# A variance over rows on one core: new tile order, last tiles shared between VectorE and ScalarE, loads split at the end, last stores from SyncE

## Chip, cores, metric

One core of one Trainium2 chip. The metric is device time in microseconds (us), median over runs. All runs compared here are of the fast state, but for one single look that is used for its trace alone.

Two words recur. A *packet* is one piece that one of the 16 DMA engines moves, 8 KB in a whole tile. A transfer has *landed* when all the DMA engines that took part in it are through, so that whoever waits for it may start.

## The reference

```python
x = np.random.randn(32, 512, 1024).astype(np.float32)
mean_sq = np.mean(x**2, axis=-1)
sq_mean = np.mean(x, axis=-1)**2
return mean_sq - sq_mean            # (32, 512): the variance of each of 16384 rows
```

67.1 MB are read, 64 KB are written.

## The kernel before

128 partitions; a tile is J = 2 rows of 1024 numbers in each partition, 1 MB, 64 tiles. Three of four tiles go to VectorE (statistics of two half rows, then an aggregate to mean and variance), one of four to ScalarE (one pass for the mean, one for the mean square, by accumulators). The order is D D D A, D for VectorE and A for ScalarE, so the very last tile is an A.

```python
J = 2; DV_FRAC = 3; XBUFS = 12; DV_CHUNK_COLS = 24; AC_CHUNK_COLS = 16
# ... cut: pools, order = D D D A, repeated

def flush_dv_chunk(lo, hi):
    res_dv = opool.tile([P, DV_CHUNK_COLS], fp32, name="res_dv")
    nc.vector.tensor_copy(out=res_dv[:, :n], in_=acc_dv[:, 1, lo:hi])          # L72
    nc.gpsimd.dma_start(out=out_t[:, lo:hi], in_=res_dv[:, :n])                # L73

def flush_ac_chunk(lo, hi):
    # tmp = mean * mean on VectorE (L79); res_ac = mean square - tmp (L83)
    nc.gpsimd.dma_start(out=..., in_=res_ac[:, :n])                            # L87

for t in order:
    xt = xpool.tile([P, J, 2, D // 2], fp32, name="xt")
    nc.sync.dma_start(out=xt, in_=src)                                         # L97
    if t < DV:
        for j in range(J):
            nc.vector.bn_stats(out=stats[:, j, 0, :], in_=xt[:, j, 0, :])      # L102
            nc.vector.bn_stats(out=stats[:, j, 1, :], in_=xt[:, j, 1, :])      # L103
            nc.vector.bn_aggr(out=acc_dv[:, :, t * J + j], in_=...)            # L104
        # ... cut: flush_dv_chunk every 24 columns
    else:
        for j in range(J):
            nc.scalar.activation(..., func=Copy, scale=1/D, accum_out=mean)            # L116
            nc.scalar.activation(..., func=Square, scale=D**-0.5, accum_out=mean_sq)   # L122
        # ... cut: flush_ac_chunk every 16 columns
```

## Time and profile before

| what | value | read from |
|---|---|---|
| time | 173.51 us (173.35 to 173.54) | runs |
| span of the profile | 171.6 us | head of the page |
| last load landed | 163.54 us | start of ScalarE's last tile in the timeline |
| VectorE, ScalarE busy | 129.1 and 74.8 us | part 1 of the page |
| DMA rate between start and tail | 416 to 428 GB/s | 40 slices |

The busy shares bound nothing here: the stream of loads runs at one rate from 5 to 161 us, and what can be won lies before and after it. The prediction shows the lines.

### The profile page before, as it was taken

How to read it: one execution, taken by the hardware profiler on the slowest of the kernel's cores; microseconds unless marked ns; L12 is line 12 of the kernel's file. 1: busy time of each engine (PE TensorE's matmuls, PEld its weight loads, DVE VectorE, ACT ScalarE, POOL GpSimd, SP SyncE). 2: the span in 40 equal slices, each digit the busy share in tenths (PEclk: the TensorE clock that was granted, in tenths of full speed). 3: DMA queues.
4: the chain of work that ended last, by engine and by line, in shares of the span. 5: the costliest groups of instructions: out<-in, count | busy, mean ns of one | idle time of the engine just before them, and what ended most of it. 6: DMA issues, size and time to landing. Idle time of an engine off the chain costs nothing.

```text
span 171.6 us, 597 instructions
## 1 busy us (share of the span) xinstructions
DVE 129.1 (75%) x296; ACT 74.8 (44%) x129; POOL 3.6 (2%) x10
## 2 busy tenths in 40 slices
DVE  0795959769695986959699793968969596995930
ACT  2009064280815528091642807346190824518082
POOL 0000000000100000000110000000010000000011
DMA  5999999999999999999999999999999999999600
GB/s 206 424 428 426 426 422 418 420 424 420 424 421 422 422 422 424 420 418 426 422 423 416 426 420 422 422 420 418 428 422 421 420 420 426 422 422 420 258 3 2
DMA packets 9412, 67.21 MB, mean 392 GB/s; under 512 B 1120, under 2 KB 1216, under 8 KB 1216
## 3 DMA queue, kind: packets, MB, share of 16 engines
q1 hardware_dynamic: 9216, 67.11, 94.0%
q0 software_dynamic: 192, 0.07, 0.2%
q14 instruction: 4, 0.03, 0.0%
HBM read 67.11 MB, written 0.07 MB: 392 GB/s over the span
## 4 chain that ended last, share of the span: by engine, by line
DMA 89%; DVE 5%; issue 3%; SPq 1%; POOLq 0%; POOL 0%
DMA xt<-in_x_dram 89%; DVE stats L102 2%; DVE stats L103 2%; SPq L97 1%; DVE acc_dv L104 1%; POOLq L157 0%; POOL out_dram L73 0%; DVE res_dv L72 0%
## 5 line engine op out<-in xcount | busy, mean ns | idle before, releaser
L102 DVE BATCH_NORM_STATS2 stats<-xt 128x6 f32<-128x512 f32 x96 | 64.1, 667 | 33.5 <-DMA xt<-in_x_dram 33.5
L116 ACT ACTIVATE garbage<-xt 128x1024 f32<-128x1024 f32 x32 | 33.8, 1057 | 91.7 <-DMA xt<-in_x_dram 91.2
L103 DVE BATCH_NORM_STATS2 stats<-xt 128x6 f32<-128x512 f32 x96 | 63.2, 658 | 0.0
L122 ACT ACTIVATE garbage<-xt 128x1024 f32<-128x1024 f32 x32 | 33.8, 1056 | 1.0
L104 DVE BATCH_NORM_AGGREGATE acc_dv<-stats 128x2 f32<-128x12 f32 x96 | 19.4, 202 | 1.6
L122 ACT ACTIVATION_READ_ACCUMULATOR garbage<-xt 128x1 f32 x32 | 6.0, 186 | 0.0
L116 ACT ACTIVATION_READ_ACCUMULATOR garbage<-xt 128x1 f32 x32 | 6.0, 186 | 0.0
L73 POOL DMA_DIRECT2D out_dram<-res_dv x4 | 2.3, 572 | 158.4 <-DVE res_dv L72 158.4
L79 DVE TENSOR_TENSOR tmp<-mean_ac 128x16 f32<-128x16 f32 x2 | 0.4, 176 | 3.0 <-ACT garbage L116 3.0
L116 ACT ACT_TABLE_LOAD x1 | 1.3, 1283 | 0.7 <-PEq L146 0.7
L87 POOL DMA_DIRECT2D out_dram<-res_ac x2 | 1.1, 538 | 7.1 <-DVE res_ac L83 7.1
L83 DVE TENSOR_TENSOR res_ac<-msq_ac,tmp 128x16 f32<-128x16 f32 x2 | 0.3, 166 | 1.0 <-ACT garbage L122 1.0
L72 DVE COPY res_dv<-acc_dv 128x24 f32<-128x24 f32 x4 | 0.7, 178 | 0.1
L146 POOL MEMSET const-float32-0.0<- 128x1 f32 x1 | 0.1, 98 | 0.2 <-issue 0.2
L146 POOL MEMSET const-bfloat16-1.0<- 128x1 bf16 x1 | 0.1, 101 | 0.0
L146 POOL MEMSET const-float32-1.0<- 128x1 f32 x1 | 0.1, 98 | 0.0
L146 POOL MEMSET const-uint8-127<- 128x1 uint8 x1 | 0.1, 98 | 0.0
## 6 DMA issues: line engine op xcount, KB each, us to landing
xt<-in_x_dram SPq DMA_DIRECT2D x64, 1024.0 KB, 19.8
out_dram<-res_dv POOLq DMA_DIRECT2D x4, 12.0 KB, 5.2
out_dram<-res_ac POOLq DMA_DIRECT2D x2, 8.0 KB, 3.3
```

The source lines that it names most:

```text
L72: nc.vector.tensor_copy(out=res_dv[:, :n], in_=acc_dv[:, 1, lo:hi])
L73: nc.gpsimd.dma_start(out=out_t[:, lo:hi], in_=res_dv[:, :n])
L79: nc.vector.tensor_tensor(out=tmp[:, :n], in0=mean_ac[:, lo:hi], in1=mean_ac[:, lo:hi], op=mybir.AluOpType.mult,)
L83: nc.vector.tensor_tensor(out=res_ac[:, :n], in0=msq_ac[:, lo:hi], in1=tmp[:, :n], op=mybir.AluOpType.subtract,)
L87: nc.gpsimd.dma_start(out=out_t[:, DV * J + lo:DV * J + hi], in_=res_ac[:, :n])
L97: nc.sync.dma_start(out=xt, in_=src)
L102: nc.vector.bn_stats(out=stats[:, j, 0, :], in_=xt[:, j, 0, :])
L103: nc.vector.bn_stats(out=stats[:, j, 1, :], in_=xt[:, j, 1, :])
L104: nc.vector.bn_aggr(out=acc_dv[:, :, t * J + j], in_=stats[:, j].rearrange("p a b -> p (a b)"),)
L116: nc.scalar.activation(out=garbage, in_=xt[:, j], func=mybir.ActivationFunctionType.Copy, scale=inv_d, accum_out=mean_ac[:, jt + j:jt + j ...
L122: nc.scalar.activation(out=garbage, in_=xt[:, j], func=mybir.ActivationFunctionType.Square, scale=inv_sqrt_d, accum_out=msq_ac[:, jt + j:j ...
L146: nc = _bacc.Bacc("TRN2", target_bir_lowering=False, num_devices=1)
```

## The change

It is meant to shorten what comes after the last load. The last A tile is shared: ScalarE takes one of its rows and VectorE the other, and so for one more tile two places before it. The last three tiles are loaded in rows, the last row in halves. A tiles now lead their groups instead of closing them. The last two stores are issued by SyncE. VectorE stores are read straight from the accumulators, without a copy. There are 16 tile buffers in place of 12.

```diff
-XBUFS = 12
+XBUFS = 16
-    for _ in range(DV_FRAC): ... D D D A ...
+    for g in range(n_act_groups):            # 13 groups: A, then 4 or 3 D
+        order.append((DV + g, False))
+        ...
+    order.append((A_last, False))
+    order.append((di, False)); di += 1
+    order.append((di, False)); di += 1
+    order.append((P_t, True))                # row 0 VectorE, row 1 ScalarE
+    order.append((Q_t, True))                # VectorE
+    order.append((R_t, True))                # row 0 ScalarE, row 1 VectorE
-        nc.vector.tensor_copy(out=res_dv[:, :n], in_=acc_dv[:, 1, lo:hi])
-        nc.gpsimd.dma_start(out=out_t[:, lo:hi], in_=res_dv[:, :n])
+        eng = nc.sync if final else nc.gpsimd
+        eng.dma_start(out=out_t[:, lo:hi], in_=acc_dv[lo // DV_CHUNK_COLS][:, 1, :])
+        if split:                            # P, Q, R
+            for j in range(J):
+                if t == R_t and j == 1:
+                    for u in range(2):
+                        nc.sync.dma_start(out=xt[:, j, u], in_=src[:, j, u])
+                else:
+                    nc.sync.dma_start(out=xt[:, j], in_=src[:, j])
+        elif t == R_t:
+            act_row(xt, 0, (t - DV) * J)
+            dve_row(xt, 1, None, special=15)     # variance straight into the tile `fin`
+            ac_cols(lo_f + 13, lo_f + 15, fin[:, 29:31], nc.vector)
+            nc.sync.dma_start(out=out_t[:, ...], in_=fin[:, 16:32])
# ... cut: the same for P with GpSimd; the middle ScalarE chunk's subtraction on GpSimd
```

More of the change, by code (lines that the diff above doesn't have):

```diff
@@ L9 @@
 J = 2
-DV_FRAC = 3
-XBUFS = 12
+XBUFS = 16
 DV_CHUNK_COLS = 24
@@ L29 @@
     T = N // (P * J)
-    if J == 1:
-        x_t = x.rearrange("b (u t) d -> t (b u) d", t=T)
-        out_t = out.rearrange("b (u t) -> (b u) t", t=T)
-    else:
-        x_t = x.rearrange("b (u t j) d -> t (b u) j d", t=T, j=J)
-        out_t = out.rearrange("b (u t j) -> (b u) (t j)", t=T, j=J)
-    DV = (T * DV_FRAC) // 4
+    x_t = x.rearrange("b (u t j) d -> t (b u) j d", t=T, j=J)
+    out_t = out.rearrange("b (u t j) -> (b u) (t j)", t=T, j=J)
+    DV = (T * 3) // 4
     AC = T - DV
@@ L44 @@
     opool = ctx.enter_context(tc.tile_pool(name="opool", bufs=8))
-    acc_dv = rpool.tile([P, 2, DV * J], fp32)
+    acc_dv = [rpool.tile([P, 2, DV_CHUNK_COLS], fp32, name=f"acc_dv{c}")
+              for c in range(DV * J // DV_CHUNK_COLS)]
     mean_ac = rpool.tile([P, AC * J], fp32)
@@ L51, with flush_dv, ac_cols @@
     inv_sqrt_d = float(D) ** -0.5
-    order = []
-    di, ai = 0, 0
-    while di < DV or ai < AC:
-        for _ in range(DV_FRAC):
-            if di < DV:
-                order.append(di)
-                di += 1
-        for _ in range(4 - DV_FRAC):
-            if ai < AC:
-                order.append(DV + ai)
-                ai += 1
-    assert sorted(order) == list(range(T))
+    n_act_groups = AC - 3
+    P_t = DV + AC - 2
+    R_t = DV + AC - 1
+    A_last = DV + AC - 3
+    d_total = DV
+    d_tail = 3
+    d_steady = d_total - d_tail
+    order = []
+    di = 0
+    for g in range(n_act_groups):
+        order.append((DV + g, False))
+        take = (d_steady + n_act_groups - 1 - g) // n_act_groups
+        for _ in range(take):
+            order.append((di, False))
+            di += 1
+    order.append((A_last, False))
+    order.append((di, False)); di += 1
+    order.append((di, False)); di += 1
+    Q_t = DV - 1
+    order.append((P_t, True))
+    order.append((Q_t, True))
+    order.append((R_t, True))
+    assert di == DV - 1
+    assert sorted(t for t, _ in order) == list(range(T))
     dv_cols_done = 0
     ac_cols_done = 0
-    def flush_dv_chunk(lo, hi):
-        res_dv = opool.tile([P, DV_CHUNK_COLS], fp32, name="res_dv")
-        n = hi - lo
-        nc.vector.tensor_copy(out=res_dv[:, :n], in_=acc_dv[:, 1, lo:hi])
-        nc.gpsimd.dma_start(out=out_t[:, lo:hi], in_=res_dv[:, :n])
-    def flush_ac_chunk(lo, hi):
+    def flush_dv(lo, hi, final=False):
+        eng = nc.sync if final else nc.gpsimd
+        eng.dma_start(out=out_t[:, lo:hi], in_=acc_dv[lo // DV_CHUNK_COLS][:, 1, :])
+    fin = rpool.tile([P, 32], fp32)
+    lo_f = AC * J - 16
+    def ac_cols(lo, hi, dst, eng):
         n = hi - lo
         tmp = opool.tile([P, AC_CHUNK_COLS], fp32, name="tmp")
-        res_ac = opool.tile([P, AC_CHUNK_COLS], fp32, name="res_ac")
-        nc.vector.tensor_tensor(
+        eng.tensor_tensor(
             out=tmp[:, :n], in0=mean_ac[:, lo:hi], in1=mean_ac[:, lo:hi],
@@ L82, in flush_ac_chunk, with flush_ac @@
         )
-        nc.vector.tensor_tensor(
-            out=res_ac[:, :n], in0=msq_ac[:, lo:hi], in1=tmp[:, :n],
+        eng.tensor_tensor(
+            out=dst, in0=msq_ac[:, lo:hi], in1=tmp[:, :n],
             op=mybir.AluOpType.subtract,
         )
-        nc.gpsimd.dma_start(
-            out=out_t[:, DV * J + lo:DV * J + hi], in_=res_ac[:, :n]
-        )
-    for t in order:
-        xt = xpool.tile([P, J, 2, D // 2], fp32, name="xt")
-        if J == 1:
-            src = x_t[t].rearrange("p (j u v) -> p j u v", j=J, u=2)
-        else:
-            src = x_t[t].rearrange("p j (u v) -> p j u v", u=2)
-        nc.sync.dma_start(out=xt, in_=src)
+    def flush_ac(lo, hi):
+        res_ac = opool.tile([P, AC_CHUNK_COLS], fp32, name="res_ac")
+        ac_cols(lo, hi, res_ac[:, :hi - lo], nc.gpsimd)
+        nc.gpsimd.dma_start(out=out_t[:, DV * J + lo:DV * J + hi],
+                            in_=res_ac[:, :hi - lo])
@@ new lines, in dve_row, with act_row @@
+    def dve_row(xt, j, col, special=None):
+        stats = spool.tile([P, 2, 6], fp32, name="stats")
+        nc.vector.bn_stats(out=stats[:, 0, :], in_=xt[:, j, 0, :])
+        nc.vector.bn_stats(out=stats[:, 1, :], in_=xt[:, j, 1, :])
+        dst = (fin[:, special:special + 17:16] if special is not None
+               else acc_dv[col // DV_CHUNK_COLS][:, :, col % DV_CHUNK_COLS])
+        nc.vector.bn_aggr(out=dst, in_=stats.rearrange("p a b -> p (a b)"))
+    def act_row(xt, j, col):
+        garbage = gpool.tile([P, 2, D // 2], fp32, name="garbage")
+        nc.scalar.activation(
+            out=garbage, in_=xt[:, j],
+            func=mybir.ActivationFunctionType.Copy,
+            scale=inv_d,
+            accum_out=mean_ac[:, col:col + 1],
+        )
+        nc.scalar.activation(
+            out=garbage, in_=xt[:, j],
+            func=mybir.ActivationFunctionType.Square,
+            scale=inv_sqrt_d,
+            accum_out=msq_ac[:, col:col + 1],
+        )
@@ new lines @@
+    for t, split in order:
+        xt = xpool.tile([P, J, 2, D // 2], fp32, name="xt")
+        src = x_t[t].rearrange("p j (u v) -> p j u v", u=2)
+        if split:
[5 more added lines that the diff above has]
+                    nc.sync.dma_start(out=xt[:, j], in_=src[:, j])
+        else:
+            nc.sync.dma_start(out=xt, in_=src)
@@ L99 @@
         if t < DV:
-            stats = spool.tile([P, J, 2, 6], fp32, name="stats")
             for j in range(J):
-                nc.vector.bn_stats(out=stats[:, j, 0, :], in_=xt[:, j, 0, :])
-                nc.vector.bn_stats(out=stats[:, j, 1, :], in_=xt[:, j, 1, :])
-                nc.vector.bn_aggr(
-                    out=acc_dv[:, :, t * J + j],
-                    in_=stats[:, j].rearrange("p a b -> p (a b)"),
-                )
-            dv_cols_done += J
-            if dv_cols_done % DV_CHUNK_COLS == 0 or dv_cols_done == DV * J:
-                lo = (dv_cols_done - 1) // DV_CHUNK_COLS * DV_CHUNK_COLS
-                flush_dv_chunk(lo, dv_cols_done)
-        else:
-            jt = (t - DV) * J
-            garbage = gpool.tile([P, 2, D // 2], fp32, name="garbage")
+                dve_row(xt, j, t * J + j)
@@ new lines @@
+            dv_cols_done += J
+            if dv_cols_done % DV_CHUNK_COLS == 0:
+                flush_dv(dv_cols_done - DV_CHUNK_COLS, dv_cols_done,
+                         final=(dv_cols_done == DV * J))
+        elif t == P_t:
+            dve_row(xt, 0, None, special=12)
+            act_row(xt, 1, (t - DV) * J + 1)
+            ac_cols(lo_f, lo_f + 12, fin[:, 16:28], nc.gpsimd)
+            ac_cols_done += J
+        elif t == R_t:
+            act_row(xt, 0, (t - DV) * J)
+            dve_row(xt, 1, None, special=15)
+            ac_cols_done += J
+            ac_cols(lo_f + 13, lo_f + 15, fin[:, 29:31], nc.vector)
+            nc.sync.dma_start(out=out_t[:, DV * J + lo_f:DV * J + AC * J],
+                              in_=fin[:, 16:32])
+        else:
@@ L115 @@
             for j in range(J):
-                nc.scalar.activation(
-                    out=garbage, in_=xt[:, j],
-                    func=mybir.ActivationFunctionType.Copy,
-                    scale=inv_d,
-                    accum_out=mean_ac[:, jt + j:jt + j + 1],
-                )
-                nc.scalar.activation(
-                    out=garbage, in_=xt[:, j],
-                    func=mybir.ActivationFunctionType.Square,
-                    scale=inv_sqrt_d,
-                    accum_out=msq_ac[:, jt + j:jt + j + 1],
-                )
+                act_row(xt, j, (t - DV) * J + j)
@@ L128 @@
             ac_cols_done += J
-            if ac_cols_done % AC_CHUNK_COLS == 0 or ac_cols_done == AC * J:
-                lo = (ac_cols_done - 1) // AC_CHUNK_COLS * AC_CHUNK_COLS
-                flush_ac_chunk(lo, ac_cols_done)
+            if ac_cols_done % AC_CHUNK_COLS == 0 and ac_cols_done < AC * J:
+                flush_ac(ac_cols_done - AC_CHUNK_COLS, ac_cols_done)
 _INS = ['x']
```

## The prediction

> **What bounds the kernel now.** I read the page from the top: the busy tenths, the DMA queues, the chain that ended last, and then the timeline of the end, because the chain turned out to follow a side branch there.
>
> ```profile
> DVE  0795959769695986959699793968969596995930
> ACT  2009064280815528091642807346190824518082
> DMA  5999999999999999999999999999999999999600
> GB/s 206 424 428 426 426 422 418 420 424 420 424 421 422 422 422 424 420 418 426 422 423 416 426 420 422 422 420 418 428 422 421 420 420 426 422 422 420 258 3 2
> ```
>
> From slice 2 to 37 the DMA engines are full and move 416 to 428 GB/s; VectorE and ScalarE both have holes. Then come about 2.5 slices of 4.29 us with no loads. So the time is three parts: a start, a stream of 67 MB at a fixed rate, and a tail. The change cannot remove bytes, so only the tail is worth anything.
>
> How deep the stream is queued is read from SyncE's own waits and from the issues:
>
> ```profile
> SPq L97 <- DMA xt<-in_x_dram: 117.2, 56, 3.0
> SPq L97 <- DVE stats L103: 2.6, 12, 0.2
> xt<-in_x_dram SPq DMA_DIRECT2D x64, 1024.0 KB, 19.8
> ```
>
> SyncE waits 56 = 64 - 8 times on an earlier load: load i is issued when load i-8 has landed. 19.8 us from issue to landing is 8 loads of 2.48 us. Eight loads in flight is the limit, not the 12 buffers; the waits on VectorE sum to 2.6 us, each of 0.2 us at most, in a queue that is 20 us ahead.
>
> The tail, from the timeline of the last microseconds:
>
> ```profile
> 163.35 0.64 DVE L103 BATCH_NORM_STATS2 stats<-xt 128x6 f32<-128x512 f32 x1
> 163.54 1.06 ACT L116 ACTIVATE garbage<-xt 128x1024 f32<-128x1024 f32 x1 [5.19 <-DMA xt<-in_x_dram]
> 164.02 0.21 DVE L104 BATCH_NORM_AGGREGATE acc_dv<-stats 128x2 f32<-128x12 f32 x1
> 164.27 0.18 DVE L72 COPY res_dv<-acc_dv 128x24 f32<-128x24 f32 x1
> ...
> 165.68 0.19 ACT L122 ACTIVATION_READ_ACCUMULATOR garbage<-xt 128x1 f32 x1
> ...
> 168.04 0.19 ACT L122 ACTIVATION_READ_ACCUMULATOR garbage<-xt 128x1 f32 x1
> 168.26 0.17 DVE L83 TENSOR_TENSOR res_ac<-msq_ac,tmp 128x16 f32<-128x16 f32 x1 [1.00 <-ACT garbage L122]
> 168.73 0.54 POOL L87 DMA_DIRECT2D out_dram<-res_ac  x1 [3.46 <-DVE res_ac L83]
> ```
>
> The last tile lands at L = 163.54, whole. It is a ScalarE tile: two rows, four passes, until 168.23 (4.69 us), while VectorE has nothing to do after 164.5. Then 0.2 us of subtraction and a store: issued 168.73, landed 1.7 us later (the issues of that window), 170.43. The span ends at 171.6, so 1.15 us of closing semaphores follow. The page's chain names DVE L72 and the store of L73, but that store had landed by 166.4; the wait that ends last is ScalarE's.
>
> The end of the stream has a second feature, in stretches of 0.2 us:
>
> ```profile
> 160.80:161.00 0.20, 0.20 (x1) 0.00 (x0) 0.00 (x0) 1.00 1.08 451
> 161.20:161.40 0.20, 0.17 (x2) 0.00 (x0) 0.00 (x0) 1.00 0.50 205
> 161.60:161.80 0.20, 0.20 (x1) 0.00 (x0) 0.00 (x0) 1.00 0.10 41
> 162.60:162.80 0.20, 0.20 (x2) 0.00 (x0) 0.00 (x0) 1.00 0.10 41
> ```
>
> After 161.5 the DMA share is about one sixteenth: one engine is 1.5 us behind the rest, and the tile does not land before it. The queue of kind "instruction" has single 8 KB packets at 31.6, 67.9, 99.4 and 101.8 us, beside the loads; such packets are my suspect for the lag, which is in every landing time above. The change does not aim at it.
>
> **What the Trainium skill says.** "DMA: Bandwidth & Descriptors", Where 436 GB/s comes from, has 435 GB/s as the fabric's ceiling; the trace's 416 to 428 agrees, so the stream has nothing to give. The same page, Why a DMA increments its semaphore by 16 and not by 1, says that a transfer counts as landed when all its engines have posted; the straggler above agrees. Its Rules for kernel authors say that issuing from several engines gives no bandwidth; so moving two stores to SyncE can only change latency. Its Anatomy of one DMA has about 2 us of fixed cost for a GpSimd-issued transfer, most of it the write receipt; the trace shows 1.7 us for an 8 KB store.
>
> **The change, part by part.**
>
> *16 buffers for 12; no copy before the VectorE stores; two small operations of the middle ScalarE chunk moved to GpSimd.* All lie beside the stream: 0. The four copies are 0.7 us of VectorE, which has 42 us of idle time.
>
> *Order: ScalarE tile first in each group, groups of 4 or 3 VectorE tiles.* A VectorE tile takes 2.65 us (156.14 to 158.8), a load 2.48. Four in a row put VectorE some 0.7 us behind, and the ScalarE tile's 2.48 us pays it back. 0 until the tail.
>
> *The tail.* Call the last landing L'. With 2.48 us for 1 MB, 1.24 for a half, 0.62 for a quarter, the landings before it are: R's third quarter L'-0.6, R row 0 L'-1.2, Q rows L'-2.5 and -3.7, P rows L'-5.0 and -6.2, two VectorE tiles L'-7.4 and -9.9. VectorE (1.33 us a row): the tile of -9.9 until -7.3, that of -7.4 until -4.6, P row 0 until -3.3, Q until -2.0 and -0.7, R's third quarter until 0.0. So it is just caught up when the last quarter comes: 0.69 (first statistics after a wait) + 0.02 + 0.21 gives L'+0.92, and with the multiplication of 0.18 L'+1.10. ScalarE has R row 0 from L'-1.24 and needs 163.54 to 165.87 = 2.33 us: L'+1.09. Both are done within 0.05 us; then the subtraction, 0.17 + 0.03: **L'+1.30**. Before, the same point was 168.44 = L+4.90. Gain 3.60 us.
>
> *The final store from SyncE.* From the end of the subtraction to GpSimd's issue 0.29 us pass (168.44 to 168.73); SyncE goes on 0.06 us after an event (chain of waits: DMA ends 15.34, next DMA 15.42 with its own event in between). Gain 0.23. Issue to landing: SyncE's first load is issued at 0.74 and the first stretch with bytes is 1.60 to 2.00, about 1.0 us; the store of GpSimd issued at 168.73 has its bytes in 169.50 to 170.00, about 1.1. Gain 0.1, so 1.6 us for the store, an estimate. The closing 1.15 us stay.
>
> *Smaller packets.* P and Q go in 4 KB runs, R's last row in 2 KB runs. An 8 KB packet takes 2.48/8 = 0.31 us of an engine. Each engine has 32 more packets and 4 more completions in the tail. At 27.2 GB/s per engine (435/16, the skill's figure) 8 KB is 0.301 us, so some 5 ns per packet are overhead: 32 x 5 ns and the completions is an estimate of 0.2 us. L' = L + 0.2.
>
> Sum: -3.60 - 0.23 - 0.1 + 0.2 = -3.73 us. 173.51 - 3.7 = **169.8 us**, a span near 167.9.
>
> **The rivals.**
>
> *A. The SyncE queue blocks the last loads.* In the source, the last VectorE store (SyncE, waits for Q's aggregate) stands before R's three loads in the same in-order queue. If built so, R's loads are issued only at about L'-0.7 of the plan and need 1.0 + 2.5 + 0.5 us: last landing 3 us late, time about 172.8. Against it: instructions are not kept in source order here. On VectorE, the next row's first statistics go before this row's aggregate (156.75 L103, 157.34 L102, 157.94 L104), that is, what is ready goes ahead of what waits. I give A 10%.
>
> *B. The straggler moves.* All landings are those of the slowest DMA engine. If the instruction packets fall on other engines, or one more falls late on the same one, L' shifts by between -1 and +0.6 us: 168.8 to 170.4. For staying put: VectorE has as many instructions as before (98 rows of 3 are 294, plus 2; before 288 + 4 + 4).
>
> *C. Short runs stream badly.* All 128 partitions read at a pitch of 512 KB; a piece of 2 or 4 KB keeps all engines in a narrower address window. For it: the first microsecond, when all engines start in step, runs at 184 to 246 GB/s. Against it: later, at 8 KB, nothing is seen. If the last 3 MB ran 10% slower, L' is 0.7 us later: 170.5.
>
> *D. The order on VectorE.* If the subtraction is put ahead of the last statistics, it makes them wait for ScalarE: 0.75 us more, about 170.5.
>
> **Range and chances.** "Faster by over 2%" needs 173.51 x 0.98 = 170.04, a gain of 3.47 us; my sum is only 0.26 us beyond it. B in its good half gives 169 and less, B's bad half, C or D end at 170.4 to 170.5, A near 172.8. I take 168.9 to 170.9 as eight in ten, and 0.60 faster, 0.39 same, 0.01 slower: nothing in it lengthens the stream by 7 us.
>
> **What would show it.** DMA tenths and GB/s as now, 8 loads in flight still, in spite of 16 buffers. In the timeline of the end: last landing at 163.7, ScalarE's last accumulator and VectorE's last aggregate within 0.2 us of each other about 1 us later, the store issued by SyncE at 165.1, landed at 166.7, span 167.9. A is shown by a gap in DMA in the last 4 us and SyncE waiting on VectorE ahead of R's loads; B by a last landing off by over 0.3 us with full rate before; C by a lower rate in the last 7 us; D by VectorE idle between the last two statistics. I am wrong in the main if ScalarE or VectorE finish over 2 us after the last landing.

## The result and the profile after

The changed kernel takes **169.41 us** (169.27 to 169.57, 8 runs; a ninth, of 169.78, is not in its median), the kernel before 173.49 us in the same rounds. The ratio is 0.9767, interval 0.9757 to 0.9776. A ratio is the mean time of one kernel's fast runs over that of the other's fast runs of the same rounds, so it is not quite the ratio of the medians quoted.

The changed kernel's page, the 40 slices (one slice is now 4.19 us):

```profile
DVE  0199599499599599599597793978959598695993
ACT  3730720720630630720723609046090632709263
DMA  5999999999999999999999999999999999999960
GB/s 203 420 426 432 422 422 420 420 418 426 420 421 422 424 420 422 422 420 422 422 421 422 424 418 418 422 424 420 420 422 419 428 416 428 416 428 409 410 236 5
```

The stream is what it was, and about one and a half slices are left after it in place of two and a half. SyncE's waits show the same limit of eight loads in flight, 53 + 5 + 2 = 60 of 68 loads waiting for an earlier one. They also show that the last VectorE store (L82) stood behind all the loads: it waited 7.0 us for VectorE, and no load waited for it.

```profile
SPq L141 <- DMA xt<-in_x_dram: 111.2, 53, 2.8
SPq L139 <- DMA xt<-in_x_dram: 10.6, 5, 2.2
SPq L82 <- DVE acc_dv L113: 7.0, 1, 7.0
SPq L137 <- DMA xt<-in_x_dram: 4.2, 2, 2.1
...
SPq L141 <- DVE stats L109: 1.2, 5, 0.4
```

The end in the timeline (start, duration, engine, line, operation):

```profile
162.60 1.06 ACT L117 ACTIVATE garbage<-xt 128x1024 f32<-128x1024 f32 x1 [1.48 <-DMA xt<-in_x_dram]
...
163.25 0.69 DVE L108 BATCH_NORM_STATS2 stats<-xt 128x6 f32<-128x512 f32 x1
...
163.92 0.69 DVE L109 BATCH_NORM_STATS2 stats<-xt 128x6 f32<-128x512 f32 x1
164.64 0.21 DVE L113 BATCH_NORM_AGGREGATE fin<-stats 128x2 f32<-128x12 f32 x1
164.74 0.18 ACT L123 ACTIVATION_READ_ACCUMULATOR garbage<-xt 128x1 f32 x1
164.96 0.16 DVE L95 TENSOR_TENSOR fin<-msq_ac,tmp 128x2 f32<-128x2 f32 x1
165.18 0.34 SPq L160 DMA_DIRECT2D out_dram<-fin  x1
```

ScalarE has its row at 162.60, 1.28 us before the last quarter lands. VectorE and ScalarE end at 164.85 and 164.92, so neither waits long for the other. To cut the end into terms I take the last landing as the end of the last packet of x in the trace's packet records (163.06 before, 163.40 after) plus 0.48 us, which is what passed before from that packet to ScalarE's start (163.06 to 163.54):

| term, us | before | after | difference | predicted |
|---|---|---|---|---|
| last landing | 163.54 | 163.88 | +0.34 | +0.2 |
| landing to end of the last subtraction | 4.90 | 1.24 | -3.66 | -3.60 |
| to the issue of the last store | 0.29 | 0.06 | -0.23 | -0.23 |
| issue to landing of that store, as SyncE sees it | 1.74 | 1.42 | -0.32 | -0.1 |
| to the end of the span | 1.11 | 1.00 | -0.11 | 0 |
| sum | 171.58 | 167.60 | -3.98 | -3.73 |

### The profile page after: what moved, and what is told of

It is laid out like the page before. It is cut to its first block, busy times and chain, and to the rows that moved or that the text cites.

```text
span 167.6 us, 597 instructions
## 1 busy us (share of the span) xinstructions
DVE 130.6 (78%) x296; ACT 65.6 (39%) x121; POOL 3.4 (2%) x12
## 4 chain that ended last, share of the span: by engine, by line
DMA 91%; DVE 3%; SPq 2%; ACT 1%; issue 0%; ACTq 0%
DMA xt<-in_x_dram 91%; SPq L141 2%; DVE stats L108 1%; DVE stats L109 1%; ACT garbage L117 1%; ACT garbage L123 1%; DVE acc_dv L113 0%; DVE fin L95 0%; ACTq L193 0%
## 5 line engine op out<-in xcount | busy, mean ns | idle before, releaser
L108 DVE BATCH_NORM_STATS2 stats<-xt 128x6 f32<-128x512 f32 x98 | 65.3, 666 | 32.7 <-DMA xt<-in_x_dram 32.7
L117 ACT ACTIVATE garbage<-xt 128x1024 f32<-128x1024 f32 x30 | 31.4, 1048 | 98.5 <-DMA xt<-in_x_dram 98.5
L109 DVE BATCH_NORM_STATS2 stats<-xt 128x6 f32<-128x512 f32 x98 | 64.4, 658 | 0.0
L123 ACT ACTIVATE garbage<-xt 128x1024 f32<-128x1024 f32 x30 | 31.2, 1041 | 0.1
L123 ACT ACTIVATION_READ_ACCUMULATOR garbage<-xt 128x1 f32 x30 | 5.6, 186 | 0.0
L117 ACT ACTIVATION_READ_ACCUMULATOR garbage<-xt 128x1 f32 x30 | 5.6, 186 | 0.0
L82 POOL DMA_DIRECT2D out_dram<-acc_dv x3 | 1.8, 586 | 106.8 <-DVE acc_dv L113 106.8
L103 POOL DMA_DIRECT2D out_dram<-res_ac x1 | 0.6, 584 | 0.3 <-POOL res_ac L95 0.3
```

The source lines that it names most:

```text
L82: eng.dma_start(out=out_t[:, lo:hi], in_=acc_dv[lo // DV_CHUNK_COLS][:, 1, :])
L103: nc.gpsimd.dma_start(out=out_t[:, DV * J + lo:DV * J + hi], in_=res_ac[:, :hi - lo])
L108: nc.vector.bn_stats(out=stats[:, 0, :], in_=xt[:, j, 0, :])
L109: nc.vector.bn_stats(out=stats[:, 1, :], in_=xt[:, j, 1, :])
L117: nc.scalar.activation(out=garbage, in_=xt[:, j], func=mybir.ActivationFunctionType.Copy, scale=inv_d, accum_out=mean_ac[:, col:col + 1],)
L123: nc.scalar.activation(out=garbage, in_=xt[:, j], func=mybir.ActivationFunctionType.Square, scale=inv_sqrt_d, accum_out=msq_ac[:, col:col ...
```

## The experiments

My theory was the sum in the prediction: nearly all the gain is the shorter work after the last landing; the rest is the store; the buffers are nothing. The rivals: the deeper buffers, the early landing alone, a latency of the store that is the same whoever issues it, and for what stays of the tail, the slow DMA engine with its cause open.

### 12 buffers in the changed kernel (e1_bufs12)

```diff
-XBUFS = 16
+XBUFS = 12
```

> The changed kernel with 12 tile buffers in place of 16. My theory: eight loads in flight are the limit, so the buffers are worth nothing: 169.4 us, within 0.15 of the changed kernel, last landing near 163.85 us, SyncE's waits on VectorE back at some 2 to 3 us in total. Rival: the deeper pool lets the load queue run further ahead and is part of the gain: 169.8 us or more.

Measured: 169.45 us, ratio 0.9771. SyncE's waits on VectorE's statistics grow from 1.6 to 2.7 us in total (two lines each), 0.4 us at most, while eight loads are queued ahead. The buffers are worth nothing.

### Last three tiles loaded whole (e2_whole_loads)

```diff
-        if split:
+        if False:
```

> The changed kernel with the last three tiles loaded whole; who computes which row stays. My theory: the last tile lands whole at about 163.55 us (no small packets), ScalarE then needs 2.33 us for its row and VectorE 1.5 us for the other, subtraction until about L+2.55, against L'+1.27 in the changed kernel with L' 0.3 us later: 0.95 us slower, 170.4 us. Rival (the split loads cost as much as they bring, because of short runs and the straggling engine): 169.4 us.

Measured: 170.77 us, 1.36 us slower than the changed kernel, where 0.95 was expected.

```profile
163.93 1.06 ACT L117 ACTIVATE garbage<-xt 128x1024 f32<-128x1024 f32 x1 [2.62 <-DMA xt<-in_x_dram]
...
166.29 0.16 DVE L95 TENSOR_TENSOR fin<-msq_ac,tmp 128x2 f32<-128x2 f32 x1 [0.64 <-ACT garbage L123]
166.51 0.34 SPq L160 DMA_DIRECT2D out_dram<-fin  x1
```

The direction and the mechanism hold: ScalarE now starts with the landing, and the subtraction ends at L + 2.52 us (expected 2.55). Two sizes were off. First, the end after the store's landing takes 1.25 us in place of 1.00. SyncE's last waits show why: after the store it walks through a list of completion counters, about 0.06 us each, and here the store's counter is the first of the list, so six more waits follow its landing, where only two do in the changed kernel.

Second, the landing in this profile, 163.93, is not earlier than with split loads. But this one execution was behind before its end began: by the completion records of the trace its 55th load landed 0.28 us later than that of the changed kernel. From that load to the last landing, the same 9 MB, it takes 22.33 to 22.36 us in the three profiles with whole loads (the kernel before, this one, e6_probe), and 22.56 to 22.58 us in the six whose loads are split as in the changed kernel and that have no instruction packet (see e5_dve_pad) in this stretch. So splitting costs the landing 0.23 us, about what I had put down for the smaller packets. Store issue 2.58 against 1.30 us after the landing, plus 0.25 of walk, less 0.23, is 1.30; measured are 1.36.

### Last two stores from GpSimd (e3_pool_stores)

```diff
-        eng = nc.sync if final else nc.gpsimd
+        eng = nc.gpsimd
-            nc.sync.dma_start(out=out_t[:, ...], in_=fin[:, 16:32])
+            nc.gpsimd.dma_start(out=out_t[:, ...], in_=fin[:, 16:32])
```

> The changed kernel with its last two stores issued by GpSimd in place of SyncE. My theory: hand-over 0.29 us in place of 0.06, issue to landing 1.7 us in place of 1.4, and perhaps 0.1 us of GpSimd's drain at the end: 0.5 to 0.65 us slower, 170.0 us. Rival (the store's latency is the write receipt, the same for both): 0.2 us slower at most.

Measured: 170.50 us, 1.1 us slower.

```profile
165.10 0.16 DVE L95 TENSOR_TENSOR fin<-msq_ac,tmp 128x2 f32<-128x2 f32 x1
165.82 0.54 POOL L160 DMA_DIRECT2D out_dram<-fin  x1 [1.60 <-DVE fin L95]
```

From the subtraction's end (165.26) to the issue pass 0.57 us in place of 0.06; the flight is 1.74 in place of 1.42; and 1.18 in place of 1.00 us follow, because SyncE again begins its walk with this store. 0.51 + 0.32 + 0.18 = 1.0. The issuing engine is thus worth about twice what I gave it; the rival (0.2 us) falls. Why GpSimd takes 0.57 us to its issue here and 0.29 in the kernel before, no run shows.

### Both rows of the last tile on ScalarE (e4_last_row_act)

```diff
-            dve_row(xt, 1, None, special=15)
+            act_row(xt, 1, (t - DV) * J + 1)
```

> The changed kernel with both rows of the last tile on ScalarE, loads split as before. My theory: ScalarE's first row ends at L'+1.07 as now and the second 2.1 to 2.35 us later, so the subtraction ends about L'+3.5 in place of L'+1.27: 2.1 to 2.3 us slower, 171.6 us: sharing the last tile is the largest single part. Rival: the early landing of the first row does most of it, and the time stays under 170.5 us.

Measured: 171.69 us, 2.3 us slower. The last subtraction ends at 167.35 us, 3.47 us after the last landing. Sharing the last tile is the largest part, and the early landing of the first row does not replace it.

### The kernel before with shared last tile alone (e8_before_shared)

```diff
+        if last:
+            for j in range(J):
+                nc.sync.dma_start(out=xt[:, j], in_=src[:, j])
-            for j in range(J):            # ScalarE
+            for j in range(J - 1 if last else J):
+            if last:                      # VectorE: row 1, variance into fin
+                nc.vector.bn_stats(...); nc.vector.bn_stats(...)
+                nc.vector.bn_aggr(out=fin[:, 15:32:16], in_=...)
# ... cut: the last ScalarE chunk's subtraction writes 15 columns of fin, which is stored
```

> The kernel before with one part of the change alone: the last tile is loaded in two rows, ScalarE takes the first, VectorE the second. Order of tiles, copies and GpSimd stores as before. My theory: in the old order VectorE has three tiles in a row just before the last one and is free only at L+0.9, so its row ends at about L+2.4 in place of the 4.9 us of before: 2.1 to 2.5 us faster than before, 171.2 us, well short of the changed kernel's 4.1 us. Rival: sharing alone is the whole gain less the store's 0.6 to 1.0 us: 170.2 us.

Measured: 171.01 us: 2.6 us faster than before, short of the changed kernel by 1.6.

```profile
164.21 0.21 DVE L115 BATCH_NORM_AGGREGATE acc_dv<-stats 128x2 f32<-128x12 f32 x1
164.33 0.12 DVE L85 TENSOR_TENSOR tmp<-mean_ac 128x15 f32<-128x15 f32 x1
164.45 0.18 DVE L73 COPY res_dv<-acc_dv 128x24 f32<-128x24 f32 x1
164.54 0.69 DVE L142 BATCH_NORM_STATS2 stats<-xt 128x6 f32<-128x512 f32 x1
...
165.85 0.21 DVE L144 BATCH_NORM_AGGREGATE fin<-stats 128x2 f32<-128x12 f32 x1
166.36 0.54 POOL L93 DMA_DIRECT2D out_dram<-fin  x1 [0.90 <-DVE fin L144]
```

ScalarE is through with its row at 164.9, as in the changed kernel. The last row has landed at 163.74, but VectorE, which in the old order has just had three tiles in a row, is busy with them until 164.42 and comes to this row only at 164.54. So the new order is not idle decoration: the last work before the store ends at 166.06 us, in the changed kernel at 165.12. These 0.94 us are the tail's order together with the second shared tile and the last row's halves, which this run does not separate. The store from GpSimd makes the other 0.7: 0.24 more to its issue, 0.26 in flight, 0.22 after its landing.

### What sets the last landing: more VectorE instructions (e5_dve_pad)

In both kernels one DMA engine was behind the others at the end: of the last load's 16 completions in the changed kernel, 15 are in by 162.70 us and the last comes at 163.85. The suspects are the packets of kind "instruction" (8 KB each), which by their name and spacing bring an engine its next instructions. These packets and the slowest packets of x beside them are, in the changed kernel:

```
instruction packets at   31.93   72.00  100.65  104.05 us
next x packet, start     32.26   72.31  100.95  104.36 us
its duration              956     687     956     720 ns   (312 is usual)
VectorE had run            50     125     181     183 instructions
```

The landing of the slowest engine fell back by 0.6 us after the first and 0.9 us after the third, the two that come 131 VectorE instructions apart, and by nothing after the others.

```diff
+            if t < DV - 3:
+                pad = ppool.tile([P, 1], fp32, name="pad")
+                nc.vector.memset(pad, 0.0)
```

> The changed kernel with 45 tiny VectorE memsets that nothing reads, at the start of VectorE's program, while it waits for the first tile. In the profiles so far VectorE had run about 50 and about 181 instructions (131 apart) when the two instruction packets came after which the slowest DMA engine fell behind by 0.6 and by 0.9 us. Theory: each such packet holds that engine up, and every landing waits for it. With 45 more instructions the packets come at 5, 180 - 45 = 135 and 310 - 45 = 265 of the old count, so a third one falls before the last load: last landing about 0.65 us later, 170.0 us. Rival: the lag has another cause (the stores, a slow engine): 169.4 us, and 3 us of VectorE work at the start costs nothing.

In the source a memset stands after each tile; in the trace all 45 ran at the start, from 0.81 to 2.25 us, before any tile had landed.

Measured: 170.39 us, ratio 0.9815 against 0.9767: 0.8 us slower by the ratios, 1.0 by the medians. The page has five instruction packets in place of four; VectorE had run 47, 181 and 310 instructions at three of them, the third at 148.96 us. By the completion records the slowest engine was 1.9 us behind the first one before this third packet and 2.9 us after it. The stretches of half a microsecond at the end (time, then VectorE, ScalarE and GpSimd busy, clock, DMA share, GB/s), first the changed kernel:

```profile
q14 instruction: 4, 0.03, 0.0%
...
162.50:163.00 0.50, 0.47 (x2) 0.40 (x1) 0.00 (x0) 1.00 0.07 29
163.00:163.50 0.50, 0.45 (x2) 0.50 (x1) 0.00 (x0) 1.00 0.04 16
163.50:164.00 0.50, 0.50 (x3) 0.47 (x3) 0.00 (x0) 1.00 0.00 0
```

then with the padding:

```profile
q14 instruction: 5, 0.04, 0.1%
...
162.50:163.00 0.50, 0.47 (x3) 0.00 (x0) 0.00 (x0) 1.00 0.06 25
...
163.50:164.00 0.50, 0.50 (x1) 0.39 (x1) 0.00 (x0) 1.00 0.06 25
164.00:164.50 0.50, 0.45 (x3) 0.50 (x1) 0.00 (x0) 1.00 0.05 20
```

A share of about one sixteenth is one engine alone; it works 1.0 us longer, to 164.42. One packet costs that engine its own 0.31 us and 0.65 us more on the packet behind it, 0.96 together; I had counted only the 0.65. The theory holds, its size was a third too small.

### Which engine is behind (e6_probe)

```diff
+        if t == R_t:
+            for k in (2, 4, 6, 8, 12, 14, 15):
+                probe = rpool.tile([P, 16], fp32, name=f"probe{k}")
+                nc.sync.dma_start(out=probe[:k, :], in_=x_t[0][:k, 0, 0:16])
# ... cut: the last three tiles are loaded whole; the last VectorE store comes from GpSimd
```

> A look at which DMA engine is the slow one; not meant to be fast. The last tile is loaded whole, and behind it on the same queue stand seven tiny loads of 2, 4, 6, 8, 12, 14 and 15 partitions, which the Trainium skill says run on the lowest-numbered 2, 4, ... 15 engines. A tiny load that includes the slow engine lands with the last tile, one without it 1.2 to 2 us earlier. Theory (one fixed engine is late): there is one k from which on all are late. Rival (all engines are late in turn, or lateness depends on the transfer): no such step.

One look, 170.6 us, its state is not known; only its trace is used. From 162.6 to 163.6 us only the late engine moves anything:

```profile
DMA packets 15, 0.02 MB, mean 17 GB/s; under 512 B 13, under 2 KB 13, under 8 KB 13
```

Two packets are its last of x. The other 13 are the tile's completion and then six pairs of a 64 B piece and its completion: it takes part in six of the seven tiny loads. The completion records have the step that was expected: the load of 2 partitions is complete at 162.79 us, that of 4 only at 164.06. If a load of k partitions runs on the lowest-numbered k engines, as the Trainium skill has it ("DMA: Bandwidth & Descriptors", Why a DMA increments its semaphore by 16 and not by 1), then it is engine 2 or 3, in the load of 4 partitions and not in that of 2. The numbering itself no run shows. So it is one engine, and all others have moved their data by 162.6.

### Variance straight from ScalarE (e7_var_bias)

```diff
-            func=Copy, scale=inv_d, accum_out=mean
+            func=Copy, scale=-inv_d * inv_sqrt_d, accum_out=neg_mean
-            func=Square, scale=inv_sqrt_d, accum_out=mean_sq
+            func=Square, scale=inv_sqrt_d, bias=neg_mean, accum_out=variance
```

> The changed kernel with ScalarE computing the variance itself: its first pass gives minus the mean in the scale of the second pass, which takes it as its bias, so that the accumulator is the variance; the multiplications and subtractions on VectorE and GpSimd go. My theory: the end is then the later of ScalarE (L'+1.07) and VectorE (L'+0.93), so the store is issued at L'+1.13 to 1.18 in place of L'+1.33: 0.15 to 0.2 us faster, 169.2 us. Rival: the second pass must wait for the first one's accumulator, which in the steady stretch is hidden but in the tail adds 0.2 us: 169.4 us.

Measured: 169.44 us, ratio 0.9759 (0.9746 to 0.9772), which the timed runs do not tell from 0.9767: inconclusive. In the profile the store is issued 1.17 us after the last landing (last packet 163.49, issue 165.14) against 1.30, so 0.13 us were won of 0.15 to 0.2; the pass with a bias takes 1.15 us in place of 1.06.

### Fewer VectorE instructions (e9_few_dve), two small things at the end (e12_tail), all together (e11_all)

```diff
# e9_few_dve
-    DV = (T * 3) // 4
+    DV = 28                  # 36 tiles for ScalarE, evenly mixed; chunks of 28 columns
# e12_tail: direct variance in the last two ScalarE rows, and
-    order.append((di, False)); di += 1
-    order.append((di, False)); di += 1
+    order.append((di, True)); di += 1
+    order.append((di, True)); di += 1
# e11_all: both
```

> The changed kernel with more tiles on ScalarE (36 in place of 16, evenly mixed; tail as it is), so that VectorE has some 176 instructions and never reaches its 181st, near which its second instruction packet came in every profile. Theory of the instruction packets: one packet of VectorE in place of two, so the slowest DMA engine lags by 0.6 to 0.8 us less, the last landing is near 163.2 us and the time 168.8 us; ScalarE gets a second packet of its own, but that falls on another engine that has slack. Rival: the lag at 100 us has another cause, 169.4 us. Third way: ScalarE, with 34 tiles of about 4.3 us in 144 us, becomes the bound and the time is 170 us or more.

Measured: 169.19 us, ratio 0.9750 (0.9737 to 0.9764): 0.2 to 0.3 us faster, not 0.65. VectorE has one instruction packet now (at 51.9 us), but ScalarE has two (31.5 and 101.8), each with a slow x packet of 688 ns behind it. The slowest engine's completions come 1.74 us after those of the first one late in the stream, against 2.1 in the changed kernel. The lag steps up by 0.4, 0.2 and 0.5 us at the three packets: the second ScalarE packet lands on an engine that then is the slowest. So one cause was traded for a smaller one of the same kind. The profile's span is 0.4 us shorter than the changed kernel's, and 0.2 of that is lost outside it: time less span is 2.0 us in all four runs of this version and 1.7 to 1.8 in all runs of the other experiments. No run shows why. The intervals of this run and the changed kernel just overlap; that the direction is right rests on this and on the padded run together.

> The changed kernel with two small things at its end. First, ScalarE's last two rows give the variance directly (as in the run with the bias), so nothing is subtracted at the end: 0.17 us. Second, two more loads are split in rows only to move the last store two places on among the eight completion counters, because SyncE, once the store has landed, walks through the rest of its waits at 0.06 us each and that place should be the last of them: 0.12 us. Together 169.15 us, against 169.4. Rival: the walk takes as long wherever the store stands, and the extra split costs what is won: 169.3 us or more.

Measured: 169.31 us, ratio 0.9757 (0.9744 to 0.9771): by the time alone not told from the changed kernel. That is the rival's number. In the profile 0.87 us follow the store's landing in place of 1.00, as expected from the last place in the walk. But the direct variance won only 0.05 us of 0.17, and the two further splits cost the landing 0.15 us: from the 55th load to the last landing it is 22.72 us here and 22.73 in e11_all, in place of 22.57.

> Both of the others together: few VectorE instructions, direct variance in the last ScalarE rows, last store at the last place of the waits. If the parts add up: 169.4 - 0.65 - 0.17 - 0.12 = 168.5 us. If the instruction packets are not the cause of the lag: 169.15 us.

Measured: **168.85 us**, ratio 0.9727 (0.9714 to 0.9740), below the changed kernel's interval and correct: the fastest version here, by 0.6 to 0.7 us, where 0.9 was expected. The shortfall is that of the lag, which at the last landing is 1.7 us in place of 2.0 (0.65 less was expected), and the 0.15 us of the two further splits.

```profile
163.74 0.69 DVE L111 BATCH_NORM_STATS2 stats<-xt 128x6 f32<-128x512 f32 x1
164.47 0.21 DVE L115 BATCH_NORM_AGGREGATE fin<-stats 128x2 f32<-128x12 f32 x1
164.73 0.19 ACT L125 ACTIVATION_READ_ACCUMULATOR garbage<-xt,mean_ac 128x1 f32 x1
165.00 0.34 SPq L163 DMA_DIRECT2D out_dram<-fin  x1
```

VectorE and ScalarE end at 164.68 and 164.92 and nothing is subtracted after them; the store is issued at 165.00.

## Why the prediction was right

169.8 was predicted, 169.41 measured, inside 168.9 to 170.9, on the side of "faster by over 2%" that had 0.60.

- *The stream is the bound and only the tail counts*: right. The rate is the same, and in the changed kernel eight loads are in flight whether there are 16 buffers or 12.
- *Landing to the last subtraction, 4.90 to 1.30*: right, 1.24 measured. The parts that were taken out one by one are all needed: without the shared tile the time is 2.3 us longer, without the split loads 1.4, and with the old order of the tail the last work ends 0.94 us later.
- *Hand-over to SyncE, -0.23*: right.
- *The final store, -0.1*: the term was mis-sized. The flight shrank by 0.32, since I put 1.6 us for a store from SyncE, by the time of its first bytes, and it took 1.42.
- *"The closing 1.15 us stay"*: wrong by 0.11 us. Its length depends on the place of the last store among SyncE's last waits.
- *L' = L + 0.2 for smaller packets*: right in size, 0.23 us by the completion records. The +0.34 between the two profiles holds 0.1 us from earlier in the stream as well. The working is not right: from the prediction's own 0.31 and 0.301 us a packet's overhead is 9 ns and not 5, and 32 of them would be 0.29 us.
- *The parts beside the stream are worth 0*: right for the buffers, by e1_bufs12. The copies left out and the subtraction moved to GpSimd were not tested alone; all that comes before the split loads has moved the landing by 0.1 us, within what profiles of the same loads differ by.
- *Rival A (SyncE blocks the last loads)*: fell; the store went behind the loads. *B (the straggler moves)*: it stayed where it was, and its suspected cause was confirmed by the padded run. *C (short runs stream badly)*: fell, with 0.23 us in place of 0.7; the last full slices show 409 and 410 GB/s. *D (the subtraction ahead of the last statistics)*: fell; it comes after the aggregate.

What stays open: why an x packet behind an instruction packet of VectorE takes 0.65 us longer and one behind ScalarE's 0.38; which engine the late one is, beyond the skill's numbering; and the 0.2 us outside the span in e9_few_dve.

## What to carry to other kernels

When a kernel streams at a fixed rate, count the time from the last landing to the end of the span in its single terms, and spread the last piece so that all engines end together soon after it lands; the order of the tiles just ahead decides whether an engine is free for it. Issue the last small store from SyncE and not from GpSimd, which was worth 1.1 us here. A transfer has landed only when the slowest DMA engine is through, and a compute engine's instruction packets can make one DMA engine the slowest: here one comes with every 130 instructions or so of VectorE, and one more of them cost 0.8 to 1.0 us.

## What the Trainium skill lacked or had wrong

- "Runtime: NRT & Kernel Launch", Instruction fetch mechanics, has refills in blocks of 16 KiB at a cost that is mostly hidden. Here they are single packets of 8 KB, some 130 instructions apart. One of VectorE's held up one DMA engine by 0.96 us, one more of them made the kernel 0.8 to 1.0 us slower, and the delay stays in every later landing.
- No page says on which DMA engine instruction packets run: VectorE's two fell on the same one, ScalarE's on another (the steps in e9_few_dve).
- "DMA: Bandwidth & Descriptors", Anatomy of one DMA, has about 2 us of fixed cost for a GpSimd-issued transfer; the 8 KB store took 1.74. It fits this cost for GpSimd alone; the store issued by SyncE took 1.42 us here. No page compares the two in the time from the end of the last input to the issue: 0.29 and 0.57 us for GpSimd, 0.06 for SyncE.
- No page has SyncE's walk at the end of a program: it goes through its completion counters at 0.06 us each, and from the last store's landing to the end of the span it took 0.87, 1.00 or 1.25 us by that store's place in the list.
